# First feed-forward product of a decoder layer: a third pair of k-tiles through seven block products, and the gated product's transposes some steps later

## The chip, the cores and the metric

One core of one Trainium2 chip. The metric is the device time of one execution in microseconds (us), the median of several runs. TensorE (PE in the profile) does matmuls, with its weight loads shown apart as PEld; VectorE is DVE, ScalarE is ACT, GpSimd is POOL, and SP is the engine whose queue issues all the DMAs of the stretch that is changed.

## The reference

One layer with 256 tokens and a model width of 2048, in float32, in three sub-layers; the change is in the third. With `x` the 256 x 2048 output of the second layer norm:

```python
def swiglu(x, w_in, w_out):
    g, u = jnp.split(x @ w_in, 2, axis=-1)      # w_in 2048 x 11264
    return (jax.nn.silu(g) * u) @ w_out         # w_out 5632 x 2048
...
y = swiglu(x, w_ffn_in[l], w_ffn_out[l])
x = layer_norm(ALPHA * x + y, ln_g[l, 2], ln_b[l, 2])
```

## The kernel before

**Numbers.** Every float32 operand of a large product is split into a high and a low part (`split`, L118: ACT writes the high part, L119, and DVE the difference, L120). A product is then three matmuls: high by high, high by low, low by high (`mm3`, L287 to L289; `chunk_mm`, L248 to L250). So one block product of a 128 x 128 piece of activations with a 128 x 512 piece of weights is three matmuls of 128 x 512.

**First feed-forward product** (L988 to L1033). The loop over `j` takes 11 blocks of 512 hidden columns. Block 0 goes through `product` (twice, gate and up). Blocks 1 to 10 have eight cells each, one for a pair `c` of k-tiles; a cell covers 2 k-tiles, 2 token tiles and 2 column blocks (gate columns and up columns). `plain_cell` (L959) loads two raw chunks of 512 KB, splits them and runs 8 block products, 24 matmuls. `fast_cell` (L932) computes the same 2 x 2 x 2 cell by seven block products, 21 matmuls, in a Strassen-Winograd scheme: sums of activation tiles come ready from a tile (`sq`) that `fast_acts` (L890) builds once, in block 0 between the gate and the up product, and sums of weight tiles are formed on DVE in each cell (L941, L942, L945, L946). Besides the split of the raw gate chunk it splits the two sum tiles `tb` and `tcs` and one half of the raw up chunk. Products m1, m5, m6, m7 gather in four PSUM banks of the pool `aux`, x11, x12, x21, x22 in four of `acc`. After the last fast cell of a block `sums` (L971) combines the m banks with one ACT copy and four DVE additions; after the last cell the gate (L1019 to L1024) adds the x banks, applies silu, multiplies and stores the two 128 x 512 results to a DRAM tile (`keep`, L215).

**Transposes of the gated product.** For blocks 0 to 6 `turn` (L175, its body `turned`, L179) is queued in `later`: its first step issues four DMAs that bring the block back in another layout (L183), its second makes four DVE transposes (L189) and an ACT copy (L190), its third a DVE subtraction (L192). `flush` advances each queued generator by one step: it is called once after a fast cell and after each of the two chunks of a plain cell, so the three steps of block j fall on the first three such calls of block j+1. The result (`hT`) is read in the second feed-forward product only. Blocks 7 to 10 are turned during the second product (`ends`).

**Order.** The cells of a block go in the order (0, 2, 3, 1, 4, 5, 6, 7), with 0 and 1 fast. Each engine runs its instructions strictly in the order that the kernel's build gave it. That order starts from the program's and is rearranged at build time by a scheduler with its own estimate of when operands are ready, so matmuls of neighbouring products and operations of neighbouring chunks interleave. `behind` (L122) adds one rule: the transposes come, on DVE, behind the last split that the program had issued before them. Buffers: 5 raw chunks, 4 split weight tiles (`hl`, each serves 12 matmuls of a plain cell), 1 `tw`, 2 `s`, 2 `turn`, 2 `tr`.

**Second product** (L1055 to L1100): two passes over 22 pairs of k-tiles, each with 6 fast cells (`fast_cell` with `hT`), the first beginning with five plain cells, the second with a fast one.

Of the kernel before, what the change touches and what calls it, by code (L numbers as in the profile page):

```python
# [11 lines left out]
F32R = mybir.dt.float32r  # L12
# [4 lines left out]
P = 128  # L17
S = 256
NT = S // P
D = 2048  # L20
# [45 lines left out]
def trunk(ctx: ExitStack, tc: tile.TileContext, a, out: bass.AP):  # L66
# [13 lines left out]
    later = []  # L80
# [9 lines left out]
    def nm(s):  # L90
        count[0] += 1
        return f"{s}_{count[0]}"
# [10 lines left out]
    def stage(dtype=F32):  # L103
        return work.tile([P, W], dtype, tag="stage", name=nm("stage"), bufs=4)
# [55 lines left out]
    def to_quad(q, tt, src):  # L160
        p = ps_aux()
        for i in range(4):
            nc.tensor.transpose(p[:, i * P:(i + 1) * P], src[:, i * P:(i + 1) * P], ident)  # L163
        sl = slice(tt * P, (tt + 1) * P)
        pv = p.rearrange("p (k t) -> p k t", k=4)
        split(q.hi[:, :, sl], q.lo[:, :, sl], pv)
# [8 lines left out]
    def turn(q, src, mixed=True, sq=None):  # L175
        q.mixed = mixed
        yield from turned(q.hi, q.lo, src, mixed, sq)
# [212 lines left out]
    for ps in wide(w_in[:, C_QI:C_KI], load_x):  # L390
        t = b8().rearrange("p (h t) -> p h t", h=8)
        for tt in range(NT):
            sl = slice(tt * P, (tt + 1) * P)
            qs = work.tile([P, 8, 2, IDIM], F32R, tag="tr", name=nm("tr"))
# [462 lines left out]
    ws = {}  # L857
# [26 lines left out]

    FAST = (0, 1)
    ORDER = (0, 2, 3, 1, 4, 5, 6, 7)

    def fast_acts():  # L890

        q = Quad()
        for t, c in enumerate(FAST):
            st = stage()
            a11, a12 = [tok[0][:, (2 * c + i) * P:(2 * c + i + 1) * P] for i in range(2)]
            a21, a22 = [tok[1][:, (2 * c + i) * P:(2 * c + i + 1) * P] for i in range(2)]
            block_sums([st[:, i * P:(i + 1) * P] for i in range(4)], a11, a12, a21, a22)
            to_quad(q, t, st)
        return q

    class Banks:

# [26 lines left out]
        sl = slice(tt * P, (tt + 1) * P)  # L929
        return q.hi[:, k, sl], q.lo[:, k, sl]  # L930

    def fast_cell(bk, act, sq, t, c, ws, stop):  # L932
        q, k = act[c * KC // 4], c * KC % 4
        a11, a12, a22 = act_of(q, k, 0), act_of(q, k + 1, 0), act_of(q, k + 1, 1)
        s1, s2, s3, s4 = [act_of(sq, i, t) for i in range(4)]
        r0, r1 = [load_chunk(w, c, q.mixed) for w in ws]
        ha, la = hl_tile()
        lows.append(split(ha, la, r0))
        hb, lb = hl_tile()
        tb = work.tile([P, 2, W], F32, tag="tw", name=nm("tw"), bufs=1)  # L940
        nc.vector.tensor_tensor(tb[:, 0], r1[:, 0], r0[:, 0], op=ALU.subtract)  # L941
        nc.vector.tensor_tensor(tb[:, 1], r1[:, 1], r1[:, 0], op=ALU.subtract)  # L942
        hc, lc = hl_tile()
        tcs = work.tile([P, 2, W], F32, tag="s", name=nm("s"))
        nc.vector.tensor_tensor(tcs[:, 0], r1[:, 1], tb[:, 0], op=ALU.subtract)  # L945
        nc.vector.tensor_tensor(tcs[:, 1], r0[:, 1], tcs[:, 0], op=ALU.subtract)  # L946
        b22 = work.tile([P, 2, W], F32R, tag="s", name=nm("s"))
        split(b22[:, 0], b22[:, 1], r1[:, 1])
        split(hb, lb, tb)
        lows.append(split(hc, lc, tcs))  # L950
        bk.mm("m1", a11, (ha[:, 0], la[:, 0]), stop)
        bk.mm("m5", s1, (hb[:, 0], lb[:, 0]), stop)
        bk.mm("m7", s3, (hb[:, 1], lb[:, 1]), stop)
        bk.mm("m6", s2, (hc[:, 0], lc[:, 0]), stop)
        bk.mm("x11", a12, (ha[:, 1], la[:, 1]))
        bk.mm("x12", s4, (b22[:, 0], b22[:, 1]))
        bk.mm("x21", a22, (hc[:, 1], lc[:, 1]))

    def plain_cell(bk, act, c, ws, stop):  # L959
        q, k = act[c * KC // 4], c * KC % 4  # L960
# [10 lines left out]
    def sums(bk):  # L971

        m = bk.t
        c11, c12, c21, c22 = [stage() for _ in range(4)]
        nc.scalar.activation(c11, m["m1"], AF.Copy)
        nc.vector.tensor_tensor(c12, c11, m["m6"], op=ALU.add)
        nc.vector.tensor_tensor(c21, c12, m["m7"], op=ALU.add)
        nc.vector.tensor_tensor(c12, c12, m["m5"], op=ALU.add)
        nc.vector.tensor_tensor(c22, c21, m["m5"], op=ALU.add)
        return c11, c12, c21, c22  # L980

    hT = []
    FAST_H = (8, 9, 10)
# [4 lines left out]
    for j in range(DFF // W):  # L988
        gs = []

        def gate(tt, p):
            g = stage()
            nc.scalar.activation(g, p, AF.Silu)
            gs.append(g)

        q = Quad()
        d = spill()
        if j == 0:
            product(x2T, [wf[:, j * W:(j + 1) * W]], seq=8, stream_seq=3, done=gate)
            side.finish()  # L1000
            sq = fast_acts()
            pu = product(x2T, [wf[:, DFF + j * W:DFF + (j + 1) * W]])
            for tt in range(NT):
                nc.vector.tensor_tensor(gs[tt], gs[tt], pu[tt], op=ALU.mult)
                keep(d, tt, gs[tt])
        else:
            ws = [wf[:, j * W:(j + 1) * W], wf[:, DFF + j * W:DFF + (j + 1) * W]]
            bk = Banks(None)
            for i, c in enumerate(ORDER):
                if c in FAST:  # L1010
                    fast_cell(bk, x2T, sq, FAST.index(c), c, ws, c == FAST[-1])
                    flush()
                    side.step(1)
                    if c == FAST[-1]:
                        cs = sums(bk)
                else:
                    plain_cell(bk, x2T, c, ws, i == len(ORDER) - 1)
            for tt in range(NT):
                g, u = cs[2 * tt:2 * tt + 2]  # L1019
                nc.vector.tensor_tensor(g, g, bk.t[f"x{tt + 1}1"], op=ALU.add)  # L1020
                nc.scalar.activation(g, g, AF.Silu)
                nc.vector.tensor_tensor(u, u, bk.t[f"x{tt + 1}2"], op=ALU.add)
                nc.vector.tensor_tensor(g, g, u, op=ALU.mult)
                keep(d, tt, g)  # L1024
        if j in FAST_H:
            t = None if j == FAST_H[0] else ffn.tile([P, D], F32R, tag="sq", name=nm("sq"), bufs=len(FAST_H) - 1)
            sqs[j] = Quad(tile=t)
        if j < 7:
            later.append(turn(q, d))
        else:  # L1030
            ends.append(turn(q, d, sq=sqs.get(j)))
        q.mixed = True
        hT.append(q)  # L1033
# [21 lines left out]
    for g, plan in enumerate(plans):  # L1055
        wo = a["w_ffn_out"][0]
        ws = [wo[:, (2 * g + n) * W:(2 * g + n + 1) * W] for n in range(2)]
        bk = Banks(None)
        held = plan[-HELD:] if g else []
        if g:  # L1060
            side.add(n3.load())
        for i, c in enumerate(plan):
            if c in held:
                break
            if c in fast_c:
                fast_cell(bk, hT, sqs[c // 2], c % 2, c, ws, c == fast_c[-1])
                flush()
                side.step(1)
            else:
                plain_cell(bk, hT, c, ws, i == len(plan) - 1)  # L1070
            if c == fast_c[-1]:
                for k, t in enumerate(sums(bk)):
                    tt, n = k // 2, 2 * g + k % 2
                    o = tok[tt][:, n * W:(n + 1) * W]
                    nc.vector.scalar_tensor_tensor(o, o, ALPHA, t, op0=ALU.mult, op1=ALU.add)
        chunks = []
        for c in held:
            for n in range(2):
                raw = load_chunk(ws[n], c, True)
                if len(chunks) < 3:  # L1080
                    hi, lo = hl_tile()
                else:
                    t = b8()
                    hi, lo = [t[:, i * KC * W:(i + 1) * KC * W].rearrange("p (k n) -> p k n", k=KC) for i in range(2)]
                lows.append(split(hi, lo, raw))
                chunks.append((c, n, hi, lo))
        for tt in range(NT):
            for c, n, hi, lo in (sorted(chunks, key=lambda x: x[1]) if tt else chunks):
                q, k = hT[c // 2], c * KC % 4
                for kk in range(KC):  # L1090
                    bk.mm(f"x{tt + 1}{n + 1}", act_of(q, k + kk, tt), (hi[:, kk], lo[:, kk]),
                          c == held[-1] and kk == KC - 1)
                side.step(1)
                if tt and c == held[-1]:
                    n3.add_to(tt, 2 * g + n, bk.t[f"x{tt + 1}{n + 1}"])
            for n in range(2):
                if not (tt and held):
                    n3.add_to(tt, 2 * g + n, bk.t[f"x{tt + 1}{n + 1}"])
            if held:
                if tt == 0:  # L1100
                    side.finish()
                n3.finish(tt)
# [24 lines left out]
```

## Time and profile before

| | |
|---|---|
| Median of 3 runs | 1465.26 us (1463.72 to 1468.70) |
| The profiled execution, its own time | 1462.86 us |
| Its span | 1460.7 us |
| PE, DVE, ACT busy | 98%, 76%, 50% of the span |
| Matmuls on PE | 6568 |
| Blocks 1 to 10 of the first feed-forward product | about 798 to 1220 us of the span |

The span is the time between the first and the last instruction of the profiled execution; its own time lies 2.2 us above that. Matmuls are pipelined, so their shown durations overlap; the distance from start to start is what one costs.

### The profile page before, as it was taken

The numbers are of one execution on the slowest core, as the hardware profiler recorded it, in microseconds if no ns is written. First come the engines' busy times: TensorE is split into PE (matmuls) and PEld (weight loads), VectorE is DVE, ScalarE is ACT, GpSimd is POOL, SyncE is SP. The second block draws the span as 40 slices with busy tenths as digits, with TensorE's granted clock in tenths as the row PEclk, the third lists the DMA queues.
The fourth block names the chain that finished last, engine by engine and source line by source line (L and its number), as shares of the span: only waits on it lengthen the run. The fifth ranks groups of instructions, "written<-read, shape, count | busy, mean of one in ns | idle before, by whom it ended". The sixth has DMA issues, their size and how long they took to land.

```text
span 1460.7 us, 18003 instructions
## 1 busy us (share of the span) xinstructions
PE 1437.2 (98%) x6568; PEld 1192.9 (82%) x6568; DVE 1110.5 (76%) x1464; ACT 729.4 (50%) x859; POOL 19.6 (1%) x43
## 2 busy tenths in 40 slices
PE   8999999999999999999989999999999999999997
PEld 7988888888888888888868888888888888887885
DVE  6575986575756666886796888888887778979777
ACT  5554456454544444545644555555455455554551
POOL 0000000000000000000000000000000000000000
PEclk9999999999999999999999999999999999999999
DMA  9884667777667779968535676767766777665762
GB/s 291 201 261 143 199 215 224 229 230 233 211 201 229 223 250 309 238 184 273 178 127 187 204 227 220 233 219 227 232 211 215 227 234 216 202 214 183 254 214 101
DMA packets 197464, 316.61 MB, mean 217 GB/s; under 512 B 18688, under 2 KB 58752, under 8 KB 197376
## 3 DMA queue, kind: packets, MB, share of 16 engines
q1 hardware_dynamic: 197376, 315.47, 69.2%
q8 instruction: 51, 0.84, 0.2%
q14 instruction: 37, 0.30, 0.1%
HBM read 298.65 MB, written 16.78 MB: 216 GB/s over the span
## 4 chain that ended last, share of the span: by engine, by line
PE 91%; DVE 4%; DMA 3%; issue 1%; ACT 0%; POOL 0%; SPq 0%; DVEq 0%; ACTq 0%
PE acc L249 14%; PE acc L250 14%; PE acc L248 14%; PE acc L289 13%; PE acc L288 13%; PE acc L287 13%; PE aux L288 3%; PE aux L289 3%; PE aux L287 3%; DVE hl L120 1%; DMA turn<-spill 1%; DVE b L775 1%; DMA raw<-in_w_ffn_out 1%; PE aux L163 0%; DMA spill<-stage 0%
## 5 line engine op out<-in xcount | busy, mean ns | idle before, releaser
L119 ACT ACTIVATE hl<-raw 128x1024 fp32r<-128x1024 f32 (+2 forms) x463 | 481.9, 1051 | 452.0 <-PE acc L250 224.6
L120 DVE TENSOR_TENSOR hl<-raw,hl 128x1024 fp32r<-128x1024 f32 (+2 forms) x463 | 554.6, 1211 | 199.1 <-ACT hl L119 198.2
L249 PE MATMUL acc<-hl,b 128*128 128x512 f32 (+1 forms) x940 | 364.6, 388 | 0.8 <-DVE hl L120 0.6
L250 PE MATMUL acc<-hl,b 128*128 128x512 f32 (+1 forms) x940 | 364.2, 387 | 0.0
L248 PE MATMUL acc<-hl,b 128*128 128x512 f32 (+1 forms) x940 | 362.4, 388 | 0.7 <-ACT b L119 0.7
L288 PE MATMUL acc<-hl,b 128*128 128x512 f32 x844 | 329.2, 391 | 0.8 <-DVE hl L120 0.8
L289 PE MATMUL acc<-hl,b 128*128 128x512 f32 x844 | 328.8, 390 | 0.0
L287 PE MATMUL acc<-hl,b 128*128 128x512 f32 x844 | 303.7, 391 | 0.0
L249 PEld LDWEIGHTS acc<-hl,b 128*128 128x128 f32 x940 | 176.6, 188 | 35.9 <-DVE hl L120 1.6
L248 PEld LDWEIGHTS acc<-hl,b 128*128 128x128 f32 x940 | 176.5, 188 | 35.3 <-ACT b L119 0.9
L250 PEld LDWEIGHTS acc<-hl,b 128*128 128x128 f32 x940 | 176.5, 188 | 35.2 <-DVE b L120 0.2
L288 PEld LDWEIGHTS acc<-hl,b 128*128 128x128 f32 x844 | 159.0, 188 | 34.8 <-DVE hl L120 1.5
L287 PEld LDWEIGHTS acc<-hl,b 128*128 128x128 f32 x844 | 159.1, 189 | 33.6 <-ACT b L119 0.2
L289 PEld LDWEIGHTS acc<-hl,b 128*128 128x128 f32 x844 | 159.0, 188 | 33.1
L189 DVE STREAM_TRANSPOSE tr<-turn 128x256 f32<-128x256 f32 (+1 forms) x148 | 67.1, 511 | 58.2 <-DMA turn<-spill 58.2
L190 ACT ACTIVATE b<-tr 128x1024 fp32r<-128x1024 f32 (+1 forms) x37 | 37.4, 1013 | 73.3 <-DVE tr L189 73.3
L119 ACT ACTIVATE hl<-s 128x1024 fp32r<-128x1024 f32 x32 | 34.0, 1062 | 42.4 <-PE acc L289 31.6
L119 ACT ACTIVATE hl<-tw 128x1024 fp32r<-128x1024 f32 x32 | 33.9, 1059 | 42.1 <-PE acc L289 32.2
L120 DVE TENSOR_TENSOR hl<-s,hl 128x1024 fp32r<-128x1024 f32 x32 | 39.1, 1223 | 12.6 <-ACT hl L119 12.3
L941 DVE TENSOR_TENSOR tw<-raw,raw 128x512 f32<-128x512 f32 x32 | 22.1, 691 | 34.8 <-DMA raw<-in_w_ffn_in 26.5
L120 DVE TENSOR_TENSOR hl<-tw,hl 128x1024 fp32r<-128x1024 f32 x32 | 39.1, 1222 | 8.2 <-ACT hl L119 8.1
L119 ACT ACTIVATE b<-aux 128x512 fp32r<-128x512 f32 (+1 forms) x50 | 26.7, 545 | 36.7 <-PE aux L163 20.5
(187 smaller groups left out, 1213.1 us busy)
## 6 DMA issues: line engine op xcount, KB each, us to landing
raw<-in_w_ffn_in SPq DMA_DIRECT2D x176, 512.0 KB, 4.8
raw<-in_w_in SPq DMA_DIRECT2D x143, 512.0 KB, 4.3
raw<-in_w_ffn_out SPq DMA_DIRECT2D x88, 512.0 KB, 4.6
raw<-in_w_out SPq DMA_DIRECT2D x32, 512.0 KB, 7.8
spill<-stage SPq DMA_DIRECT2D x56, 256.0 KB, 2.4
turn<-spill SPq DMA_DIRECT2D x104, 128.0 KB, 4.0
raw<-in_w_o_dsa SPq DMA_DIRECT2D x16, 512.0 KB, 4.3
raw<-in_w_o_moba SPq DMA_DIRECT2D x16, 512.0 KB, 4.6
```

Of the source, the lines that this page charges most:

```text
L119: nc.scalar.activation(hi, src, AF.Copy)
L120: return (eng or nc.vector).tensor_tensor(lo, src, f(hi), op=ALU.subtract)
L189: nc.vector.transpose(tr[:, i, :], v[:, i])
L190: nc.scalar.activation(hi, tr, AF.Copy)
L248: nc.tensor.matmul(o[:, :n], xh, hi[:, kk, :n], start=k == 0, stop=False)
L249: nc.tensor.matmul(o[:, :n], xh, lo[:, kk, :n], start=False, stop=False)
L250: nc.tensor.matmul(o[:, :n], xl, hi[:, kk, :n], start=False, stop=k == kts - 1)
L287: nc.tensor.matmul(o, lh, rh, start=start, stop=False)
L288: nc.tensor.matmul(o, lh, rl, start=False, stop=False)
L289: nc.tensor.matmul(o, ll, rh, start=False, stop=stop)
L775: prev = nc.vector.scalar_tensor_tensor(t, t, scalar, self.rows[row][:, j * W:(j + 1) * W], op0=op0, op1=op1)
L941: nc.vector.tensor_tensor(tb[:, 0], r1[:, 0], r0[:, 0], op=ALU.subtract)
```

## The change

A third pair of k-tiles (cell 2) of blocks 1 to 10 becomes a fast cell, so the order of a block is (0, 3, 1, 4, 2, 5, 6, 7) with 0, 1 and 2 fast. `fast_acts` builds a second tile of activation sums for it, in the pool that has two such tiles for the second product. Inside a fast cell the program's order of the products is m1, x11, m5, m7, x12, m6, x21, except in the first cell of a block or pass, where it stays m1, m5, m7, m6, x11, x12, x21; this holds for the second product too. The turning of blocks 0 to 6 goes through `late`. As `late` is written, its first step issues the DMAs and stops, and after four stops in all the fifth step makes the transposes, the sixth the subtraction; before, those were the second and the third step.

```diff
-    FAST = (0, 1)
-    ORDER = (0, 2, 3, 1, 4, 5, 6, 7)
+    FAST = (0, 1, 2)
+    THIRD = 1
+    ORDER = ((0, 2, 3, 1, 4, 5, 6, 7), (0, 3, 1, 4, 2, 5, 6, 7))
...
-        q = Quad()
+        qs = []
         for t, c in enumerate(FAST):
+            if t == 0:
+                qs.append(Quad())
+            elif t == 2:
+                qs.append(Quad(tile=ffn.tile([P, D], F32R, tag="sq", name=nm("sq"), bufs=2)))
...
-            to_quad(q, t, st)
-        return q
+            to_quad(qs[t // 2], t % 2, st)
+        return qs
...
-    def fast_cell(bk, act, sq, t, c, ws, stop):
+    def fast_cell(bk, act, sq, t, c, ws, stop, pairs=True):
...
+        for name in ("m1 x11 m5 m7 x12 m6 x21" if pairs else "m1 m5 m7 m6 x11 x12 x21").split():
+            bk.mm(name, *todo[name])
...
+    def late(gen, n):
+        next(gen)
+        for _ in range(n):
+            yield
+        yield from gen
...
-            for i, c in enumerate(ORDER):
-                if c in FAST:
-                    fast_cell(bk, x2T, sq, FAST.index(c), c, ws, c == FAST[-1])
+            fast = FAST if j >= THIRD else FAST[:2]
+            for i, c in enumerate(ORDER[len(fast) - 2]):
+                if c in fast:
+                    fast_cell(bk, x2T, sq[c // 2], c % 2, c, ws, c == fast[-1], i > 0)
...
-            later.append(turn(q, d))
+            later.append(late(turn(q, d), 4))
...
-                fast_cell(bk, hT, sqs[c // 2], c % 2, c, ws, c == fast_c[-1])
+                fast_cell(bk, hT, sqs[c // 2], c % 2, c, ws, c == fast_c[-1], i > 0)
```

## Rows read from the trace of the kernel before

**Rows 1.** The page: span, and busy time of each engine.

```profile
span 1460.7 us, 18003 instructions
...
PE 1437.2 (98%) x6568; PEld 1192.9 (82%) x6568; DVE 1110.5 (76%) x1464; ACT 729.4 (50%) x859; POOL 19.6 (1%) x43
```

**Rows 2.** Busy time by stretch: two blocks, the second product's start, its passes' seam.

```profile
core 0: us, PE busy (x) PEld busy (x) DVE busy (x) ACT busy (x) POOL busy (x), PEclk, DMA share, GB/s
882.53:924.77 42.24, 42.24 (x187) 34.92 (x187) 36.34 (x44) 22.19 (x24) 0.00 (x0) 1.00 0.69 224
...
1093.73:1135.97 42.24, 42.24 (x187) 34.92 (x187) 33.52 (x39) 21.61 (x23) 0.00 (x0) 1.00 0.65 212
1218.10:1260.50 42.40, 42.40 (x189) 35.09 (x188) 41.57 (x56) 23.66 (x24) 0.00 (x0) 1.00 0.75 219
1330.00:1340.00 10.00, 7.89 (x33) 5.59 (x32) 10.00 (x14) 3.07 (x3) 0.00 (x0) 1.00 0.54 177
```

**Rows 3.** PE in order of time: first m1 matmul of two blocks in succession.

```profile
919.81 0.39 PE L287 MATMUL aux<-hl,b 128*128 128x512 f32 x1
...
962.05 0.39 PE L287 MATMUL aux<-hl,b 128*128 128x512 f32 x1
```

**Rows 4.** DVE in order of time, that block: start, us, instructions, [idle before].

```profile
927.05 0.68 DVE L941 TENSOR_TENSOR tw<-raw,raw 128x512 f32<-128x512 f32 x1
927.65 0.68 DVE L942 TENSOR_TENSOR tw<-raw 128x512 f32<-128x512 f32 x1
930.39 2.17 DVE L189 STREAM_TRANSPOSE tr<-turn 128x256 f32<-128x256 f32 x4 [2.06 <-DMA turn<-spill]
932.49 0.65 DVE L945 TENSOR_TENSOR s<-raw,tw 128x512 f32<-128x512 f32 x1
...
936.53 1.22 DVE L120 TENSOR_TENSOR hl<-tw,hl 128x1024 fp32r<-128x1024 f32 x1
937.66 1.22 DVE L120 TENSOR_TENSOR hl<-s,hl 128x1024 fp32r<-128x1024 f32 x1
938.80 2.35 DVE L120 TENSOR_TENSOR hl<-raw,hl 128x1024 fp32r<-128x1024 f32 x2
...
945.73 2.51 DVE L120 TENSOR_TENSOR hl<-raw,hl 128x1024 fp32r<-128x1024 f32 x2
951.75 0.69 DVE L941 TENSOR_TENSOR tw<-raw,raw 128x512 f32<-128x512 f32 x1 [3.51 <-DMA raw<-in_w_ffn_in]
...
963.01 1.29 DVE L1023 TENSOR_TENSOR stage<-stage,stage 128x512 f32<-128x512 f32 x2
```

**Rows 5.** Whole run by line and shape: count, busy, mean ns, idle before.

```profile
L120 DVE TENSOR_TENSOR hl<-raw,hl 128x1024 fp32r<-128x1024 f32 x453 | 546.4, 1219 | 186.5 <-ACT hl L119 185.6
L119 ACT ACTIVATE hl<-raw 128x1024 fp32r<-128x1024 f32 x453 | 474.4, 1058 | 442.2 <-PE acc L250 223.3 <-PE acc L289 145.4 <-PE aux L289 16.6
L942 DVE TENSOR_TENSOR tw<-raw 128x512 f32<-128x512 f32 x32 | 21.9, 684 | 0.0
L119 ACT ACTIVATE s<-raw 128x512 fp32r<-128x512 f32 x32 | 20.0, 626 | 21.9 <-DMA raw<-in_w_ffn_in 16.2 <-PE acc L289 4.6 <-DMA raw<-in_w_ffn_out 0.7
```

**Rows 6.** Waits, 838 to 1260 us: total us, times, longest; the last row SP's queue.

```profile
ACT hl L119 <- PE acc L289: 123.3, 91, 2.1
...
DVE tw L941 <- DMA raw<-in_w_ffn_in: 22.9, 9, 3.5
...
DVE tr L189 <- DMA turn<-spill: 10.5, 6, 2.9
...
SPq L921 <- DVE hl L120: 190.7, 102, 6.6
```

**Rows 7.** Block 0: activation sums on DVE, the idle after them, PE's transposes.

```profile
765.89 0.28 DVE L206 TENSOR_TENSOR stage<-b 128x128 f32<-128x128 f32 x1
...
767.10 0.49 DVE L209 TENSOR_TENSOR stage<-b,stage 128x128 f32<-128x128 f32 x2
773.81 1.23 DVE L120 TENSOR_TENSOR hl<-raw,hl 128x1024 fp32r<-128x1024 f32 x1 [6.22 <-ACT hl L119]
...
775.71 0.82 PE L163 MATMUL aux<-ident,stage 128*128 128x128 f32 x6
```

**Rows 8.** Waits at the seam of the second product's passes.

```profile
PEld acc L287 <- DVE b L756: 1.7, 1, 1.7
```

More of the change, by code (lines that the diff above doesn't have):

```diff
@@ L950, in fast_cell @@
         lows.append(split(hc, lc, tcs))
[L951 to L957, printed above, removed]
+        todo = {"m1": (a11, (ha[:, 0], la[:, 0]), stop), "m5": (s1, (hb[:, 0], lb[:, 0]), stop),
+                "m7": (s3, (hb[:, 1], lb[:, 1]), stop), "m6": (s2, (hc[:, 0], lc[:, 0]), stop),
+                "x11": (a12, (ha[:, 1], la[:, 1])), "x12": (s4, (b22[:, 0], b22[:, 1])),
+                "x21": (a22, (hc[:, 1], lc[:, 1]))}
+        for name in ("m1 x11 m5 m7 x12 m6 x21" if pairs else "m1 m5 m7 m6 x11 x12 x21").split():
+            bk.mm(name, *todo[name])
     def plain_cell(bk, act, c, ws, stop):
@@ L1008, in trunk @@
             bk = Banks(None)
-            for i, c in enumerate(ORDER):
-                if c in FAST:
-                    fast_cell(bk, x2T, sq, FAST.index(c), c, ws, c == FAST[-1])
+            fast = FAST if j >= THIRD else FAST[:2]
+            for i, c in enumerate(ORDER[len(fast) - 2]):
+                if c in fast:
+                    fast_cell(bk, x2T, sq[c // 2], c % 2, c, ws, c == fast[-1], i > 0)
                     flush()
                     side.step(1)
-                    if c == FAST[-1]:
+                    if c == fast[-1]:
                         cs = sums(bk)
                 else:
-                    plain_cell(bk, x2T, c, ws, i == len(ORDER) - 1)
+                    plain_cell(bk, x2T, c, ws, i == 7)
             for tt in range(NT):
```

## The prediction

> **What bounds the kernel now.** I read the page first, then busy time by stretch, then PE and DVE in order of time through one block, then the waits.
>
> The page says that PE works through the whole span and DVE three quarters of it [rows 1]. Since shown matmuls overlap, 98% alone proves little; the beat proves it. A block starts with its first m1 matmul at 919.81 and the next one at 962.05 [rows 3]: 42.24 us for 6 plain cells of 24 and 2 fast ones of 21 matmuls, 186 in all, so 0.2271 us for one, at the full granted clock (PEclk 1.00, the 2.4 GHz level, [rows 2]). In the two blocks shown PE has no gap. ACT's main wait is for PE to free a split-weight tile, 123.3 us between 838 and 1260 [rows 6]: both vector engines are held back by PE, not the reverse. So **blocks 1 to 10 are bound by PE, and a matmul taken out there is worth its 0.2271 us as long as DVE keeps up**. How close DVE is, is the question: in blocks 1 to 7, which also turn an earlier block, it is busy 36.34 of 42.24 us; in blocks 8 to 10 only 33.5 [rows 2].
>
> **The change, part by part.**
>
> *Matmuls.* In 10 blocks one plain cell becomes fast: 10 x 3 = 30 matmuls less, 30 x 0.2271 = 6.81 us, a block of 183 being 41.56 us.
>
> *The third cell's activation sums.* One tile, made once in block 0. On DVE eight small sums, made for two cells now, run from 765.89 to 767.6 us, so the third cell adds about 0.9 us and a 512-column split (0.60 below); DVE then idles 6.22 us, which covers it [rows 7]. PE pays: four transposes more, of which six take 0.82 us [rows 7], so 4 x 0.14 = 0.55 us, I write 0.6. Without DVE's cover it would be 1.5 us once.
>
> *DVE in a block.* Start to start, a split of 1024 columns takes 1.13 us (936.53 to 937.66) and a 512-column operation 0.60 (927.05 to 927.65) [rows 4]. A fast cell has three of the former and five of the latter: 3 x 1.13 + 5 x 0.60 = 6.39 us. A plain one has two splits, 2.26 us. So each block gains 4.13 us of DVE work: 40.5 us of 41.56 in blocks 1 to 7, 37.7 in 8 to 10. It fits, with 1.1 us to spare instead of 5.9.
>
> The rule against this is in the Trainium skill, "VectorE: DVE Perf Modes", section "The DRAIN you can't avoid": the next operation starts only when the pipe of the one before is empty, unless it is one that isn't held. Taken that way each operation costs its whole duration. The trace disagrees: neighbours start 1.13 us apart where one lasts 1.22 [rows 4]. What it would give is a rival below.
>
> *ACT.* Three splits and a half-size one instead of two: 1.06 + 0.63 = 1.7 us more [rows 5] on 22.2 of 42.24 [rows 2]; hidden. POOL gets nothing. SP's queue issues the same 16 raw loads per block, and the turn's four DMAs still go out at the first step, past no other transfer; moved are only DVE's four transposes, ACT's copy and DVE's subtraction.
>
> *The transposes' place.* As written they come at the fifth flush, not the second: three steps later. Now DVE stands in front of them waiting for their DMA, 2.06 us in the block shown, 10.5 in six blocks [rows 4, 6], with the splits behind them in its queue. Three flushes on, some 10 us, the data is there: that wait goes, and I count it as DVE room, not as time, for PE has no gap there. Nobody waits for the later result, which the second product alone reads.
>
> *Does DVE reach the third fast cell in time?* The gate of the block before ends on DVE at 963.01 + 1.2, 2.2 us into the block [rows 3, 4]. From there to the end of the third fast cell's preparation it must do: a plain cell (2.26), a fast one (6.39), a plain one (2.26), the turn (2.10 + 1.13) and a fast one (6.39), 20.5 us, ending at 22.7. With the new order inside the cell PE needs the last split, for m6, after 90 matmuls of earlier cells and 15 of this one, at 105 x 0.2271 = 23.8 us. Slack 1.1. The old block gives the scale of stray waits: there two plain cells, the turn and a fast one make 14.1 us, plus the 2.06 wait 18.4, and the split was done at 938.9, at 19.1 us [rows 3, 4]: 0.7 of others. Slack left 0.4: tight, but not late. The stretch that begins the second product shows that it can be done: DVE busy 41.57 of 42.40 us, PE without a gap [rows 2].
>
> *The wait that stays.* Before the next block's first fast cell DVE waits 3.51 us for that cell's second raw chunk, 2.5 on average [rows 4, 6]. It harms nothing now. SP can only issue a load when DVE has released a raw chunk [rows 6], so when DVE falls behind, it finds the chunk landed; I take what is left of the wait to fit into the 1.1 us. Bounds: no stall, or the wait kept whole (rival 2).
>
> *Order of products in fast cells of the second product.* PE is full there except at the seam of the two passes, where it is busy only 7.89 of 10 us, waiting for DVE to empty the x banks [rows 2, 8]. The new order makes m6 of the last fast cell later, hence the sums; or, with later deadlines, DVE freer. Bounds: 2.1 us gained, about 1.4 lost (six matmuls later). I take 0, having nothing nearer.
>
> **Sum.** -6.81 + 0.6 = -6.2 us. The profiled execution took 1462.86 us (span 1460.7 [rows 1] and 2.2 around it), so 1456.7 on its scale; it lies 2.4 below the median of the runs, 1465.26, so **1459.1 us** on the median's. 0.3%, 4.4 us, is about what a measurement of this kernel can tell from no change.
>
> **The rivals.**
>
> 1. *DVE is a little late.* The slack of 0.4 us is missed by about half a microsecond in each of the blocks 1 to 7: 7 x 0.5 = 3.5 back, 1462.6 us. For it: three fast cells within five put 20.5 us of DVE work against 21.6 of PE's, and only four split tiles separate them. Against it: DVE's 98% stretch above.
>
> 2. *DVE becomes the bound: slower.* Its place is the seam from one block to the next. The wait for the second raw chunk stays, since that load waits for a split of the block's last plain cells, and DVE, in its fixed order, has the weight differences next. At 3.0 us kept, blocks 1 to 7 take 40.5 + 3.0 = 43.5 us, 1.3 more than now; 7 x 1.3 - 3 x 0.68 + 0.6 = +7.7: 1473.0 us. It decides from 2.0 us of waits per block on (1.1 of room and 0.9 that eats the gain). For it: the wait is there in most blocks [rows 6]. Against it: it comes while DVE is ahead.
>
> 3. *Whole durations count.* By rows 5, 20 splits of 1.22, 25 half-size operations of 0.684 and 2.2 of transposes are 43.7 us a block: +1.5 x 7 - 2.0 + 0.6 = +9.1, 1474.4 us. This is what the Trainium skill's drain rule named above would make of it. The same sum for the kernel before gives 39.0, where 36.3 were measured [rows 2].
>
> 4. *The transposes don't leave their wait*, because the build's order places them right behind the split before them, and the spill's way back is as late: 10.5 / 6 = 1.75 us of wait on 40.5 is 42.2 in seven blocks, so only 30 matmuls' worth in blocks 8 to 10 remains: -2.0 + 0.6 = -1.4, 1463.8 us.
>
> 5. *The seam's gap closes* by the new order of products: 2.1 more, 1457.0 us.
>
> **How the numbers follow.** Forecast 0.52, rival 1 0.18, rival 2 0.17, rival 3 0.03, rival 4 0.05, rival 5 0.05. The forecast's own range is 1457.5 to 1461.0, 1.6 to 1.9 us each way, half or so of the spread of the three runs (-1.5 to +3.4), since it is for a median; nine tenths of it lie below 1460.9 us, the bound of faster, together with rival 5 and a little of rival 1: 0.53. Slower, above 1469.7, are rival 3 and most of rival 2: 0.17. The rest, 0.30, is within 0.3%. The range reaches from 1456.0 (below rival 5) to 1468.0, past rivals 1 and 4 and into the small end of rival 2; what lies outside it is most of rivals 2 and 3.
>
> **What would show it.** Right: from m1 to m1, blocks 1 to 10 take 41.56 us, PE without a gap; DVE busy some 40 us in blocks 1 to 7; no wait of the transposes for the turn's DMA; 6568 matmuls become 6542 (30 fewer, four transposes more). Wrong: blocks 1 to 7 at 42 us or more with PE waiting on L120 in the third fast cell (rival 1), or DVE idle before L941 for 2 us or more while PE waits at the block's start (rival 2). Blocks 8 to 10 longer than 41.56 would break the price of a matmul itself.

## The result

The changed kernel takes 1485.20 us (1483.45 to 1493.75, four runs) against 1464.49 of the kernel before in the same session: a ratio of 1.0149 (95% interval 1.0128 to 1.0171). It is 20.7 us slower where 5.4 faster was forecast, and lies far outside the range.

The page of the changed kernel, first:

```profile
span 1482.4 us, 18037 instructions
...
PE 1443.2 (97%) x6542; PEld 1185.8 (80%) x6542; DVE 1150.1 (78%) x1529; ACT 746.3 (50%) x880; POOL 19.0 (1%) x43
```

The matmuls went from 6568 [rows 1] to 6542, as forecast. The loss is in the blocks of the first feed-forward product. Busy time by stretch, block 4 and block 8, each from one block's first m1 matmul to the next, after two stretches around a gap of PE that come in below (columns as in [rows 2]):

```profile
830.00:870.00 40.00, 37.17 (x153) 29.34 (x153) 33.71 (x42) 20.12 (x23) 0.00 (x0) 0.96 0.58 187
858.50:861.70 3.20, 3.13 (x7) 2.48 (x8) 3.20 (x5) 0.26 (x1) 0.00 (x0) 0.50 0.52 164
926.58:971.47 44.89, 43.14 (x184) 33.97 (x183) 40.36 (x50) 24.27 (x27) 0.00 (x0) 1.00 0.66 212
1107.08:1151.82 44.74, 44.24 (x195) 36.18 (x194) 39.95 (x48) 25.06 (x28) 0.00 (x0) 1.00 0.66 221
```

Where the kernel before took 42.24 us per block [rows 2, 3] and PE now has 41.56 of work, a block takes 44.9, and PE has gaps. DVE is busy 40.36 us in block 4, 0.1 from the 40.5 forecast: **the amount was right, and DVE still stands idle 4.5 us in that block**. Below, "block length" is the distance between the first x12 matmul of the third fast cell in one block and in the next, a mark that each block has once: 44.89 us on average from block 1 to 7, 43.13 from 8 to 10 (the step from 7 to 8 is in neither). (The stretch of block 8 above is longer than that because it holds 195 matmuls: the build lets neighbouring blocks interleave.) The latter have nothing to transpose.

Who waits for whom between 790 and 1225 us (total us, times, longest):

```profile
DVE tw L946 <- DMA raw<-in_w_ffn_in: 24.9, 17, 3.9
...
DVE tr L189 <- DMA turn<-spill: 12.7, 6, 2.7
...
PE acc L288 <- DVE hl L120: 6.6, 9, 2.1
```

The third row is new: PE waits for a low part on DVE. (It counts only what the overlapping records leave uncovered; the starts of matmuls that lie more than 0.3 us apart lose 26 us in all from 830 to 1240, beyond 0.2271 each.) The first two say what DVE waits for. The first of them is no longer than in the kernel before, whose row for the same stretch is

```profile
DVE tw L941 <- DMA raw<-in_w_ffn_in: 26.5, 11, 3.5
```

There the wait cost PE nothing. What has changed is what stands behind it.

In order of time on DVE, first in block 4 and at the seam to block 5, then in block 8 (L946 and L947 are the weight differences that were L941 and L942, L1033 and L1034 the gate that was L1022 and L1023):

```profile
933.82 1.29 DVE L1034 TENSOR_TENSOR stage<-stage,stage 128x512 f32<-128x512 f32 x2
...
944.47 2.16 DVE L189 STREAM_TRANSPOSE tr<-turn 128x256 f32<-128x256 f32 x4 [1.90 <-DMA turn<-spill]
...
973.22 1.22 DVE L120 TENSOR_TENSOR hl<-s,hl 128x1024 fp32r<-128x1024 f32 x1
975.65 0.69 DVE L946 TENSOR_TENSOR tw<-raw,raw 128x512 f32<-128x512 f32 x1 [1.21 <-DMA raw<-in_w_ffn_in]
976.26 0.68 DVE L947 TENSOR_TENSOR tw<-raw 128x512 f32<-128x512 f32 x1
976.86 1.28 DVE L1033 TENSOR_TENSOR stage<-stage,acc 128x512 f32<-128x512 f32 x2
...
978.66 1.22 DVE L120 TENSOR_TENSOR hl<-raw,hl 128x1024 fp32r<-128x1024 f32 x1
...
1119.69 1.23 DVE L120 TENSOR_TENSOR hl<-s,hl 128x1024 fp32r<-128x1024 f32 x1
1123.45 0.69 DVE L946 TENSOR_TENSOR tw<-raw,raw 128x512 f32<-128x512 f32 x1 [2.54 <-DMA raw<-in_w_ffn_in]
1124.06 0.69 DVE L947 TENSOR_TENSOR tw<-raw 128x512 f32<-128x512 f32 x1
1124.66 1.22 DVE L120 TENSOR_TENSOR hl<-raw,hl 128x1024 fp32r<-128x1024 f32 x1
```

and PE at the same moment of block 8:

```profile
1124.37 1.07 PE L287 MATMUL acc<-hl,b 128*128 128x512 f32 x4
1125.94 0.50 PE L288 MATMUL acc<-hl,b 128*128 128x512 f32 x1 [0.50 <-DVE hl L120]
```

Read the two together: at 1120.9 DVE has nothing in front of it but the third cell's weight difference, which needs that cell's second raw chunk. It waits 2.54 us, does the two differences, and only then makes the low part of the plain chunk that PE needs first; PE starts the chunk's high parts (L287) and stops at the first low one (L288). The raw chunk that it waited for was issued at 1118.07, when DVE had ended the second fast cell's split of 1116.81, and landed 5.3 us later. At 975.65 the same happens with the second fast cell: in front of the gate and of two plain splits.

In blocks 3 to 7 this is the smaller part. Of the 3.3 to 3.7 us that a block's gaps take there, 2.8 to 2.9 lie in the third fast cell and right behind it, where PE waits for that cell's own parts. In block 4, first DVE, then PE:

```profile
955.34 1.23 DVE L120 TENSOR_TENSOR hl<-s,hl 128x1024 fp32r<-128x1024 f32 x1 [1.18 <-ACT hl L119]
```

```profile
952.47 0.50 PE L288 MATMUL acc<-s,sq 128*128 128x512 f32 x1 [0.46 <-DVE s L120]
...
953.60 0.50 PE L288 MATMUL aux<-hl,sq 128*128 128x512 f32 x1 [0.40 <-DVE hl L120]
...
955.36 0.50 PE L287 MATMUL aux<-hl,sq 128*128 128x512 f32 x1 [0.55 <-ACT hl L119]
```

The cell's last split ends 30.0 us into the block (955.34 + 1.23 against 926.58), where 22.7 was forecast and 23.8 was the need.

The queue of SP around the turn in block 4 (DMA issues in order of time):

```profile
934.54 0.95 SPq L215 DMA_DIRECT2D spill<-stage  x2
936.28 0.38 SPq L926 DMA_DIRECT2D raw<-in_w_ffn_in  x1
939.46 2.52 SPq L183 DMA_DIRECT2D turn<-spill  x4
942.07 12.47 SPq L926 DMA_DIRECT2D raw<-in_w_ffn_in  x6
```

The gate ends 8.5 us into the block (933.82 + 1.29 against 926.58) instead of 2.2 [rows 3, 4], the store follows, the turn's DMAs wait for the store, and the transposes, though three flushes later in the program, wait 2.1 us a block, against 1.75 before [rows 6]. The third cell's raw loads stand behind those DMAs. So the third cell is late by 6.3 us of the gate and 3.6 of waits behind it (0.47, 1.90 and 1.18), less 2.6 us of work that was done ahead of the gate: 7.3 us, from 22.7 to 30.0.

### The profile page after: what moved, and what is told of

It is laid out like the page before. It is cut to its first block, busy times and chain, and to the rows that moved or that the text cites. A ratio compares the mean times of both kernels' runs of the same rounds, so it can differ in the third digit from the quotient of the medians.

```text
span 1482.4 us, 18037 instructions
## 1 busy us (share of the span) xinstructions
PE 1443.2 (97%) x6542; PEld 1185.8 (80%) x6542; DVE 1150.1 (78%) x1529; ACT 746.3 (50%) x880; POOL 19.0 (1%) x43
## 4 chain that ended last, share of the span: by engine, by line
PE 73%; DVE 11%; DMA 10%; issue 2%; ACT 1%; SPq 1%; POOL 0%; DVEq 0%; ACTq 0%
PE acc L249 14%; PE acc L250 14%; PE acc L248 14%; PE acc L288 8%; PE acc L289 8%; PE acc L287 8%; DMA raw<-in_w_ffn_in 5%; DVE hl L120 4%; DMA spill<-stage 2%; PE aux L288 2%; PE aux L289 2%; DMA raw<-in_w_in 2%; PE aux L287 2%; ACT hl L119 1%; SPq L183 1%
## 5 line engine op out<-in xcount | busy, mean ns | idle before, releaser
L120 DVE TENSOR_TENSOR hl<-raw,hl 128x1024 fp32r<-128x1024 f32 (+2 forms) x453 | 543.2, 1210 | 178.1 <-ACT hl L119 176.4
L119 ACT ACTIVATE hl<-raw 128x1024 fp32r<-128x1024 f32 (+2 forms) x453 | 470.8, 1051 | 411.7 <-PE acc L250 223.6
L288 PE MATMUL acc<-hl,b 128*128 128x512 f32 x784 | 308.4, 394 | 7.3 <-DVE hl L120 6.9
L289 PE MATMUL acc<-hl,b 128*128 128x512 f32 x784 | 306.1, 391 | 0.0
L287 PE MATMUL acc<-hl,b 128*128 128x512 f32 x784 | 276.9, 393 | 1.6 <-ACT hl L119 1.6
L250 PEld LDWEIGHTS acc<-hl,b 128*128 128x128 f32 x940 | 176.5, 188 | 35.5 <-DVE b L120 0.2
L248 PEld LDWEIGHTS acc<-hl,b 128*128 128x128 f32 x940 | 176.5, 188 | 35.2 <-ACT b L119 0.9
L249 PEld LDWEIGHTS acc<-hl,b 128*128 128x128 f32 x940 | 176.6, 188 | 34.9 <-DVE hl L120 0.7
L288 PEld LDWEIGHTS acc<-hl,b 128*128 128x128 f32 x784 | 148.2, 189 | 44.9 <-DVE hl L120 14.0
L287 PEld LDWEIGHTS acc<-hl,b 128*128 128x128 f32 x784 | 147.9, 189 | 35.9 <-ACT hl L119 5.0
L289 PEld LDWEIGHTS acc<-hl,b 128*128 128x128 f32 x784 | 148.2, 189 | 30.7
L119 ACT ACTIVATE hl<-s 128x1024 fp32r<-128x1024 f32 x42 | 44.6, 1061 | 79.1 <-DVE s L951 39.0
L120 DVE TENSOR_TENSOR hl<-s,hl 128x1024 fp32r<-128x1024 f32 x42 | 51.4, 1224 | 17.0 <-ACT hl L119 16.6
L119 ACT ACTIVATE hl<-tw 128x1024 fp32r<-128x1024 f32 x42 | 44.6, 1061 | 38.4 <-PE acc L289 21.7
L946 DVE TENSOR_TENSOR tw<-raw,raw 128x512 f32<-128x512 f32 x42 | 28.9, 688 | 34.8 <-DMA raw<-in_w_ffn_in 24.9
L120 DVE TENSOR_TENSOR hl<-tw,hl 128x1024 fp32r<-128x1024 f32 x42 | 51.3, 1221 | 3.4 <-ACT hl L119 3.3
```

The source lines that it names most:

```text
L119: nc.scalar.activation(hi, src, AF.Copy)
L120: return (eng or nc.vector).tensor_tensor(lo, src, f(hi), op=ALU.subtract)
L248: nc.tensor.matmul(o[:, :n], xh, hi[:, kk, :n], start=k == 0, stop=False)
L249: nc.tensor.matmul(o[:, :n], xh, lo[:, kk, :n], start=False, stop=False)
L250: nc.tensor.matmul(o[:, :n], xl, hi[:, kk, :n], start=False, stop=k == kts - 1)
L287: nc.tensor.matmul(o, lh, rh, start=start, stop=False)
```

## The experiments

The expectations name four theories. **A**: DVE, which works in order, has about 1 us of room left per block, so every wait at its head now reaches PE: the one for the turn's DMA, and the ones for raw chunks, which come late because there are only five raw buffers. **B**: the amount of DVE work alone is too much. **C**: the new order of products inside a fast cell does it. **D**, formed after the runs on buffers, cell order and queue: the build's order puts the fast cells' weight differences, which wait for a second raw chunk, ahead of plain chunks' splits and of the gate.

The table gives device time, the ratio to the kernel before in the same session, and mean block lengths (blocks 1 to 7, with a turn; 8 to 10, without). In the kernel before, by its second fast cell, the steps are 42.24 but for two: 43.60 from block 1 to 2, with 192 matmuls instead of 186 between the marks, and 42.82 with a small gap. The marks of other runs, too, have a few matmuls more or fewer than 183 between them in single blocks.

| run | us | ratio (interval) | 1 to 7 | 8 to 10 |
|---|---|---|---|---|
| changed kernel | 1485.20 | 1.0149 (1.0128 to 1.0171) | 44.89 | 43.13 |
| third_only | 1493.70 | 1.0189 (1.0155 to 1.0223) | 46.48 | 42.95 |
| three_no_late | 1491.29 | 1.0173 (1.0131 to 1.0214) | 45.99 | 42.62 |
| raw6 | 1471.34 | 1.0040 (1.0002 to 1.0078) | 42.66 | 41.86 |
| raw6_late9 | 1476.63 | 1.0075 (1.0051 to 1.0099) | 42.84 | 41.63 |
| raw6_nopairs | 1473.86 | 1.0075 (1.0024 to 1.0127) | 42.25 | 41.78 |
| order122 | 1474.87 | 1.0073 (1.0038 to 1.0109) | 43.75 | 41.62 |
| turn_after_f2 | 1492.79 | 1.0185 (1.0152 to 1.0218) | 45.87 | 43.33 |
| diff_behind | 1472.74 | 1.0055 (1.0040 to 1.0070) | 43.18 | 41.62 |
| raw6_diff_behind | 1473.45 | 1.0061 (1.0044 to 1.0078) | 43.70 | 41.63 |
| o122_diff_behind | 1462.22 | 0.9976 (0.9959 to 0.9994) | 41.78 | 41.63 |
| o122_rule_first | 1458.99 | 0.9965 (0.9951 to 0.9980) | 41.74 | 41.63 |
| o122_rule_no_late | 1492.46 | 1.0194 (1.0168 to 1.0220) | 46.63 | 41.62 |
| o122_rule_no_pairs | 1460.89 | 0.9976 (0.9963 to 0.9989) | 41.72 | 41.62 |

### The change's parts one by one

*third_only*: transposes at the second flush and the old order of products, so that the third fast cell alone is left.

```diff
-            later.append(late(turn(q, d), 4))
+            later.append(turn(q, d))
...
-... c == fast[-1], i > 0)
+... c == fast[-1], False)
```

> The third fast cell alone: products in the old order inside a cell, transposes at the second flush as before. Theory A (DVE, strictly in order, has about 1 us of room per block; every wait at its head - the turn's DMA, a raw chunk - now reaches PE): blocks 2 to 7 again near 45 us (44 to 46.5), blocks 8 to 10 near 43.5, total 1481 to 1490 us. Rival B (the amount of DVE work alone is too much): the same, but with DVE idle under 1 us a block. Rival C (the new order of products inside a cell is what costs): 1458 to 1466 us, blocks at 41.6.

*three_no_late*: only the first of these two lines.

> The changed kernel with the transposes back at the second flush. Theory A: the move gained nothing, since the wait went along with it: 1482 to 1488 us, DVE's wait for the turn's DMA 1.5 to 4 us a block. If the move did help as it was meant to: 1490 us or more. If it is the move that costs: below 1475 us.

*two_late*: two fast cells as before (`THIRD = 99`), old order of products, later transposes.

> Two fast cells as before, only the transposes three flushes later. Theory A: blocks stay at 42.24 us, 1464.5 us within 2, and DVE's wait for the turn's DMA falls from 1.8 us a block to under 0.5, since here the store goes out early in the block. If the later transposes themselves cost something: blocks above 42.5, 1467 us or more.

The third fast cell alone brings all of the loss and more (1493.70, above the 1481 to 1490 expected); the new order of products and the later transposes each give a little back, within each other's intervals, and 1491.29 us for three_no_late falls where the later transposes were said to help. C falls. The waits that come first in third_only are not those of the changed kernel (790 to 1225 us):

```profile
DVE tr L189 <- DMA turn<-spill: 25.5, 7, 4.3
...
PE acc L288 <- DVE hl L120: 19.8, 10, 3.5
DVE tw L946 <- DMA raw<-in_w_ffn_in: 19.7, 15, 3.9
```

So which wait reaches PE differs from setting to setting, as A has it. Some of the loss of third_only is PE's clock: 25 of its matmuls in blocks 1 to 10 start 0.43 us apart behind a gap, 5 us in all, against six and 1.2 us in the changed kernel.

The later transposes alone are neutral: two_late took 1464.72 us, ratio 1.0000 (0.9985 to 1.0014). But one expectation was missed: DVE's wait for the turn's DMA did not go, it was 11.2 us in six blocks. Moving the transposes three flushes does not by itself bring them behind their DMA. With two fast cells that wait and 30.7 us in 18 times at the differences leave PE all but full.

### Buffers, cell order, queue

*raw6*: a sixth raw buffer, its room taken from the second `turn` buffer. *raw6_late9*: with it, `late(..., 9)`. *raw6_nopairs*: with it, the old order of products.

```diff
-name=nm("raw"), bufs=5)
+name=nm("raw"), bufs=6)
...
-NTURN = 2
+NTURN = 1
```

> The changed kernel with six raw chunk buffers instead of five (one turn buffer less, to make room). Theory A: the second raw chunk of the third fast cell no longer waits for the fast cell before it: blocks 8 to 10 fall from 43.5 to 41.6-42.2 us, blocks 2 to 7 from 44.9 to 43-44.3 us, total 1473 to 1481 us. Rival B: no block shorter by more than 0.3 us, 1483 us or more.

> Six raw buffers, the transposes five flushes later still, behind the third fast cell. Theory A: the 0.5 to 0.9 us that PE still waits per block behind the transposes goes; blocks 2 to 7 from 42.6 to 41.7-42.1 us, total 1465 to 1469 us. Rival B (DVE's amount): blocks stay at 42.6, 1470 to 1473 us.

> Six raw buffers, old order of products inside all fast cells. Theory A: the split weights of a fast cell are then needed up to 1.4 us earlier, so PE waits more where it already waits: blocks 2 to 7 at 43 to 44 us, total 1473 to 1481 us. If the order of products is worth nothing: 1470 to 1473 us.

*order122*: one, two and two plain cells behind the fast ones instead of one, one and three; *raw6_order122*: this with six buffers.

```diff
-(0, 3, 1, 4, 2, 5, 6, 7))
+(0, 3, 1, 4, 5, 2, 6, 7))
```

> The changed kernel, five raw buffers, but the plain cells between the fast ones dealt out 1, 2, 2 instead of 1, 1, 3 (cells 0, 3, 1, 4, 5, 2, 6, 7). Theory A (the third fast cell's second raw chunk waits for a buffer that the second fast cell holds): with one more plain cell in between it does not; blocks 8 to 10 at 41.6-42.3 us, blocks 2 to 7 at 42.5-44, total 1466 to 1476 us. If the number of raw buffers helped for another reason (more loads in flight in general): blocks no shorter than 44 us, 1481 us or more.

> Six raw buffers and the plain cells dealt out 1, 2, 2. Theory A: both ways out of the same wait together; blocks 8 to 10 at 41.6 us as with the order alone, blocks 2 to 7 at 41.9-42.7, total 1463 to 1469 us. If six buffers and the order do the same thing and nothing more: 1469 to 1472 us, as with six buffers alone.

*turn_after_f2*: `late` replaced by a generator that yields eight times before the turn's first step. *pool_queue*: stores and turn DMAs of the feed-forward part issued from GpSimd's queue.

> Five raw buffers; the whole turn, its four DMAs too, eight flushes later, behind the third fast cell, so that no raw load of the fast cells stands behind the turn's DMAs on the issuing queue. Theory A has two waits in blocks 2 to 7, raw buffers and the turn: this takes the second away, blocks 2 to 7 fall from 44.9 to what blocks 8 to 10 take, 43 to 44 us, blocks 8 to 10 stay at 43 to 44.5, total 1475 to 1481 us. If the raw buffers are all of it: no change, 1483 us or more; if the queue is all of it: below 1470 us.

> The changed kernel, five raw buffers, with the stores of the gated product and the turn's DMAs issued from GpSimd's queue instead of SP's, from the first feed-forward product on. If raw loads that stand behind them on SP's queue are what delays DVE in blocks 2 to 7: from 44.9 to 43-44 us there and no change in blocks 8 to 10, total 1474 to 1480 us. If it is the number of raw buffers alone: blocks unchanged within 0.5 us, 1482 us or more.

A sixth buffer gave back 14 us and the new order of cells 10, as A wanted, and in blocks 8 to 10 either brings, to 0.3 us, the length that PE's work asks for. With six buffers, transposes moved still further (raw6_late9, 1476.63 us against 1465 to 1469 expected) do not help, and the old order of products (raw6_nopairs) costs nothing that can be told from the scatter. Had it stopped there, "five buffers are too few" would have been the story. But the two together took 1495.09 us (1.0208, 1.0186 to 1.0229), with blocks of 45.8; clearing SP's queue gave 1499.61 (1.0238, 1.0218 to 1.0259), and taking the turn out of the way 1492.79. What these have in common stands in the waits, first of raw6, then of raw6_order122, then of pool_queue (790 to 1225 us; the line number shifts by two in the last):

```profile
DVE tw L946 <- DMA raw<-in_w_ffn_in: 19.2, 15, 2.6
PE acc L288 <- DVE hl L120: 3.4, 7, 0.8
```

```profile
DVE tw L946 <- DMA raw<-in_w_ffn_in: 30.5, 13, 6.1
PE acc L288 <- DVE hl L120: 17.3, 11, 2.7
```

```profile
DVE tw L948 <- DMA raw<-in_w_ffn_in: 56.0, 28, 5.1
PE acc L290 <- DVE hl L120: 26.2, 11, 3.7
```

In these three, the longer the weight differences wait at the head of DVE, the longer PE waits for a low part. It is no rule: turn_after_f2, with 34.7 us at the differences, has 12.6 in that row and 7.2 more for high parts of fast cells, from ACT. And in raw6_order122, pool_queue and turn_after_f2 5 to 10 us of the loss are again matmuls 0.43 us apart behind the longer gaps. Each of these edits also gave the build other readiness times, and with them another order on DVE, so none of them changed one thing alone.

### The order on DVE

The order that the build gave DVE in the changed kernel is, at the seam between two blocks (number on DVE, line, what is written; raw and hl numbers rise in the order in which PE uses the chunks):

```
823 L120  hl_7865<-s_7866
824 L946  tw_7952<-raw_7946,raw_7944     second fast cell
825 L947  tw_7952<-raw_7946
826 L1033 stage_7732 (gate)
...
829 L120  hl_7911<-raw_7909              plain chunk, used before that cell
...
832 L120  hl_7928<-raw_7926              plain chunk, used before that cell
834 L120  hl_7948<-raw_7944              that cell's own first split
```

*diff_behind* adds one rule of order and changes nothing else in the program: on DVE the two differences come behind the last split that the program issued before them, that of their own cell's first chunk.

```diff
-        nc.vector.tensor_tensor(tb[:, 0], r1[:, 0], r0[:, 0], op=ALU.subtract)
-        nc.vector.tensor_tensor(tb[:, 1], r1[:, 1], r1[:, 0], op=ALU.subtract)
+        with behind():
+            nc.vector.tensor_tensor(tb[:, 0], r1[:, 0], r0[:, 0], op=ALU.subtract)
+            nc.vector.tensor_tensor(tb[:, 1], r1[:, 1], r1[:, 0], op=ALU.subtract)
```

> The changed kernel, five raw buffers, with one rule of order more: in a fast cell the two weight differences come, on DVE, behind the split of that cell's first raw chunk, so never ahead of a plain chunk's split that PE needs sooner. Work, buffers, loads and queues are the same. Theory D (the build's order puts the differences ahead of plain chunks' splits and of the gate; they wait there for the cell's second raw chunk, and what PE needs next waits behind them): PE's waits for L120 in plain cells go, blocks 8 to 10 fall from 43-44.7 to 41.6-42.3 us, blocks 2 to 7 from 44.9 to 42-43, total 1461 to 1470 us. Theory A in its narrow form (the five raw buffers themselves set the pace): no block shorter by more than 0.5 us, 1480 us or more.

*raw6_diff_behind* and *o122_diff_behind*: the rule with six buffers, and with the cells dealt out 1, 2, 2.

> The same rule with six raw buffers. Theory D: little is left for the sixth buffer to do, blocks 41.6-42.2 us, total 1459 to 1466 us, at or below the kernel before. Theory A in its narrow form: as six buffers alone, 1470 to 1473 us.

> The same rule, five raw buffers, plain cells dealt out 1, 2, 2. Theory D: blocks 41.6-42.5 us, total 1459 to 1467 us, and no longer scattered as the two runs with that order and without the rule were (43.6 with five buffers, 45 with six). If that order needs something else: 1470 us or more.

With five buffers and the same work the rule takes 12.5 us off. DVE's waits for raw chunks at the differences vanish from the list, and blocks 8 to 10 stand at 41.62: A in its narrow form, that five buffers set the pace, falls. D holds for those blocks; for the whole it promised more, 1461 to 1470 us. The rule also moves other operations, since the build arranges DVE's order anew around it: in the changed kernel plain splits stand between the operations of one fast cell, in diff_behind these come in one run. What is shown is that the order on DVE alone was worth 12.5 us, not which exchange in it. A sixth buffer on top gives nothing, as D said, though 1473.45 misses the 1466 expected for it. What is left of diff_behind is in blocks 1 to 7, and there the list shows (790 to 1225 us):

```profile
PE aux L287 <- ACT hl L119: 3.2, 6, 0.6
DVE tr L189 <- DMA turn<-spill: 2.3, 4, 1.1
```

PE waits for the third fast cell's own weights, m6's `hl` last: the tight place of the prediction. With a plain cell more ahead of it (o122_diff_behind) it is gone too: 41.63 us in every block but one, and 1462.22 us, below the kernel before.

### What the parts are worth in the right order

*o122_rule_first*: as o122_diff_behind, but the rule in the first product only (`with behind() if act is x2T else nullcontext()`); *o122_rule_no_late* and *o122_rule_no_pairs* undo one part of the change in o122_diff_behind.

> As o122_diff_behind, the rule of order in the first product alone; the second product as in the changed kernel. Theory D: blocks stay at 41.63 us; the seam of the second product's passes goes back from 3.7 us of gaps to 1.7; total 1458 to 1462 us, below the kernel before clear of noise. If the rule in the second product cost nothing: 1462 us again.

> As o122_diff_behind, but the transposes back at the second flush. If the later transposes are needed for the third fast cell: blocks 2 to 7 at 42.2 to 44 us, total 1466 to 1474 us, DVE waiting 1 to 3 us a block for the turn's DMA. If the order of the differences is all: blocks at 41.6-41.8, 1460 to 1464 us.

> As o122_diff_behind, with the old order of products inside the fast cells. If DVE now has room: blocks at 41.6-41.8 us, and the seam shorter by up to 1.5 us, total 1459 to 1463 us. If the later deadlines of the new order are needed: blocks 2 to 7 over 42.2, 1466 us or more.

o122_rule_first is the fastest, 0.35% below the kernel before; its interval overlaps those of o122_diff_behind and o122_rule_no_pairs. Its blocks 4 and 9:

```profile
920.52:962.15 41.63, 41.63 (x185) 34.35 (x184) 40.36 (x50) 23.86 (x27) 0.00 (x0) 1.00 0.71 228
1128.65:1170.28 41.63, 41.63 (x185) 34.35 (x183) 37.36 (x45) 23.03 (x26) 0.00 (x0) 1.00 0.72 228
```

PE without a gap, and DVE busy the same 40.36 us as in the changed kernel's 44.89, so B falls. On DVE in block 4, plain splits first, then the differences, without a wait (the inserted line makes L946 L947):

```profile
925.41 2.35 DVE L120 TENSOR_TENSOR hl<-raw,hl 128x1024 fp32r<-128x1024 f32 x2
927.68 0.68 DVE L947 TENSOR_TENSOR tw<-raw,raw 128x512 f32<-128x512 f32 x1
...
934.90 2.21 DVE L189 STREAM_TRANSPOSE tr<-turn 128x256 f32<-128x256 f32 x4 [0.56 <-DMA turn<-spill]
```

At the seam of the second product's passes the gaps are 1.8 us, against 3.7 in o122_diff_behind and some 2.4 before: there the rule costs about 2 us.

The later transposes are needed after all: without them 1492.46 us, blocks 1 to 7 at 46.6, and the waits of o122_rule_no_late are

```profile
DVE tr L189 <- DMA turn<-spill: 23.6, 7, 4.0
PE acc L288 <- DVE hl L120: 19.3, 6, 3.7
```

one gap of PE of 3 to 3.9 us per block, right behind a wait of the transposes, and behind most of these gaps a stretch at the lower clock (39 matmuls 0.43 us apart, 7.8 us in all). The expectation was 1466 to 1474; the size was missed. The new order of products inside a cell is worth nothing here: 1460.89 us without it, intervals overlapping.

### Two more tries

*raw6_o122_off*: six buffers, the 1, 2, 2 order, and the turn's subtraction and the gate's last multiplications on GpSimd instead of DVE. *third_from_8*: `THIRD = 8`, the 1, 2, 2 order for those blocks, transposes at the second flush; the new order of products stays.

> As raw6_order122, with 2.3 us of DVE's work per block moved to GpSimd (the turn's subtraction in blocks 1 to 7, the gate's last multiplication). Theory A with DVE's room as the measure: room grows from about 1.1 to 3.4 us a block, what waits are left fit into it, blocks 2 to 7 at 41.6-42.0 us, total 1458 to 1464 us, the first below the kernel before. If GpSimd's operations are so slow that the store and the buffers come late, or slow DVE down: blocks over 42.5, 1467 us or more.

> The third fast cell only in blocks 8 to 10, where nothing is turned, there with the cells dealt out 1, 2, 2; five raw buffers, transposes where they were. Theory A: blocks 1 to 7 at 42.24 us, 8 to 10 at 41.6, 1463.1 us against 1464.5, within 0.3% of the kernel before; if the waits come back with that order behind two-fast-cell blocks: above 1466 us.

The first took 1525.15 us (1.0422, 1.0396 to 1.0448) where 1458 to 1464 was expected: SP's queue waited 72.7 us in 16 times for GpSimd's multiplication in front of a store, with raw loads behind it, and the differences on DVE waited 37.5 us between 790 and 1225. Less DVE work does not help where the order holds it up. The second took 1463.80 (1.0004, 0.9989 to 1.0018), the same as before, as expected.

## Why the prediction was wrong

*The price of a matmul.* Right. 183 matmuls took 41.63 us in the runs without gaps, 41.56 were worked out; rival 3 (whole durations on DVE, 43.7 us) cannot be, since 41.63 holds all of DVE's work. So the trace went against the Trainium skill's drain rule ("VectorE: DVE Perf Modes", "The DRAIN you can't avoid") as rival 3 took it; it agrees with what that section excepts, that an operation which isn't held starts earlier.

*DVE's amount.* Right: 40.5 forecast, 40.36 measured, and PE can be full beside it.

*The wait that stays.* **This step failed.** It said: "when DVE falls behind, it finds the chunk landed; I take what is left of the wait to fit into the 1.1 us." The chunk had not landed, because its buffer is released by DVE itself, one fast cell earlier; and the wait was not one per block but stood ahead of the second and third fast cell too, 24.9 us in 17 times, 0.75 to 1.7 us at a time in blocks 2 to 7 and up to 3.9 in blocks 8 to 10. In total these waits were no longer than before (26.5 in 11 times); with 1.1 us of room in place of 5.9 they reached PE. I had read "its fixed order" for the seam alone (rival 2) and never asked what the build would put in front of what when three cells, not two, ask for two chunks at once. Rival 2 had the mechanism; its price, 1473.0, was 12 us too low, because it counted one wait per block and left out what the waits do to blocks 8 to 10, the gate, the turn and the third fast cell.

*The transposes' place.* "That wait goes" failed too: I moved the transposes, and held the store and the turn's DMAs still. The gate moved back six us, because the build put it on DVE behind the first fast cell's last splits and the second one's differences (these wait 1.21 us at the seam to block 5; in block 4 DVE has no wait in the 8.5 us up to the gate's end, only work put ahead of it), and the wait went along: 12.7 us in six blocks, as rival 4 had it. "Past no other transfer" was true of the turn's DMAs and missed that the third cell's raw loads now come behind them. How much of the loss is the queue's own stays open: the run that cleared it changed DVE's order as well.

*The third fast cell in time.* **This step failed too**: "tight, but not late" was late by 7.3 us on DVE in block 4, since the sum began at a gate that ends 2.2 us into the block and allowed 0.7 us for stray waits. The sign named for rival 1, PE waiting in the third fast cell, is where 2.8 to 2.9 us of each of the blocks 3 to 7 went, over half of all the gaps; rival 1's price, half a microsecond a block, was far too small. Even with the rule of order and the cells still 1, 1, 3, PE loses 1.5 us per block there. How the lateness divides between the waits and the work that the build put ahead of that cell stays open.

*Sums for the third cell, the seam.* The 0.6 us can't be told from the scatter of the runs' starts (the first block begins between 792.5 and 796.8 us in different runs). The seam lost nothing in the changed kernel: its one larger gap is 1.7 us.

That o122_rule_first lands on the forecast's 1459.1 us says that the sum was one for a kernel in the right order, not that the forecast was nearly right; that kernel has another order of cells and a rule that the forecast did not know of.

## What to carry to other kernels

When an engine that runs in order goes from 86 to 97% busy, price its waits, not its work: list what stands at the head of its queue whenever it waits, who released that, and what the slowest engine needs from behind it. Before adding buffers, look at the built order; one line of order was worth as much as a buffer here, and an edit that changes the schedule changes everything at once, so a gain from one setting (six buffers: 14 us) may turn into a loss with the next (with another cell order: 20 us slower than without).

## What the runs showed of the hardware

DVE can be busy 40.36 of 41.63 us, operations starting 1.13 us apart where each lasts 1.22, with PE full and no contention to be seen. With GpSimd in the place of DVE for one multiplication of 128 x 512 SP's next store waited 4.5 us on average (72.7 us in 16), GpSimd's own waits included; where DVE does it, in the changed kernel, SP waited 4.1 us in 18 times (790 to 1225 us). And once in the changed kernel a gap of PE was followed by a lower clock: behind the gap of 2.1 us that ends at 858.57, seven matmuls start 0.43 us apart instead of 0.2271, at a granted clock of 0.50, the 1.2 GHz level (the windows of the changed kernel, second row; 0.96 over the 40 us around it, first row). Gaps of 0.5 to 1.6 us in the later blocks left it at 1.00. The length of the gap alone did not decide: in o122_rule_no_late the stretch right behind a gap of 3.4 us stayed at 1.00 (first row), and a little behind another of the same length PE fell to the lower level (second row).

```profile
858.64:862.00 3.36, 3.35 (x15) 2.78 (x16) 3.36 (x4) 1.64 (x2) 0.00 (x0) 1.00 0.67 181
904.85:908.20 3.35, 3.35 (x9) 2.63 (x8) 3.35 (x4) 0.55 (x1) 0.00 (x0) 0.51 0.94 282
```
